# The opening of a hybrid trunk kernel: six blocks of S5's input per piece instead of four

## The chip, the cores and the metric

The kernel runs on one core of a Trainium2 chip. The metric is the device time of one execution in microseconds (us); three runs of the kernel before gave 919.19 us as their median, 918.78 and 919.51 us as the ends. The core has five engines with a queue of their own each, worked off in order: TensorE (PE; its weight loads are listed as PEld), VectorE (DVE), ScalarE (ACT), GpSimd (POOL) and SyncE (SP), which here does little but issue DMAs. They meet through semaphores. A DMA may be issued by SP, by ACT or by POOL.

## The reference

One layer of a decoder trunk with 256 positions and a model width of 2048. The part that matters here is the normalisation, the input projection and what the S5 branch takes from it:

```python
def hybrid_layer(x, mem, pre_g, ...):
    h = rms_norm(x, pre_g)
    proj = h @ w_in
    a_u, a_v, a_g, b_x, b_g, x_q, x_g, gate_logits = jnp.split(proj, splits, axis=-1)
    y_a = spatial_gating(a_u, a_v, sg_ln_g, sg_ln_b, sg_w, sg_b) * jax.nn.silu(a_g)
    y_b = s5_branch(b_x, a_re, a_im, log_dt, b_re, b_im, c_re, c_im, d, glu_w, glu_b) * jax.nn.silu(b_g)
    y_x = memory_cross_attention(x_q, rms_norm(mem, mem_g), xa_wk, xa_wv) * jax.nn.silu(x_g)
    ys = jnp.stack([y_a, y_b, y_x], axis=2)
    branch = jnp.einsum('bsnc,ncd->bsnd', ys, w_branch)
    gates = jax.nn.sigmoid(gate_logits.reshape(bsz, seq, N_BRANCH, D_MODEL))
    merged = jnp.sum(gates * branch, axis=2)
    out = merged @ w_out
    return x + rms_norm(out, post_g)
```

`b_x`, the input of S5, has 1024 columns: eight blocks of 128. Each block is a product of a [2048, 128] strip of `w_in` with `h`, so it is summed over 16 slices of 128 model channels. Everything is in float32.

## The kernel before

Every product is made from two halves of each factor. `split_to` (lines 92 to 94) casts a weight tile to float32r on ACT, the high half `hi`, and subtracts that from the source on DVE, which leaves the low half `lo`; `norm_split` (158 to 167) does the same with a slice of `x`, scaled by the gain `g_pre` on the way. The row's own norm is applied later. `cm_mm` (169 to 174) then issues two matmuls for one block of 128 columns and one slice k: one of 512 columns (the weight's high half against both halves of the slice) and one of 256 columns (the weight's low half against the slice's high half). For the first slice the 512 comes first, for all others the 256.

The program starts with eight matmuls on zeros (`wps`, lines 244 to 247), which belong to no result. Then comes the opening. Eight pieces `pc` hold two slices each, k = 2pc and 2pc + 1. A row of a piece has, for each slice, 256 columns of `x` (transposed) and 512 columns of `w_in`, which are S5's blocks 0 to 3. The first three pieces are loaded slice by slice into the three buffers named `raw`, the others in one DMA each, all of them issued by SP; the very first slice comes as two DMAs, its `x` and its weights. The gains (`vecs`) come by a DMA that ACT issues. For each slice ACT scales (`x`, line 165) and casts (`hl`, line 93), DVE does the two low halves (lines 166 and 94), and PE adds the slice to the four blocks, which lie in two accumulators in PSUM, `acc0[0]` and `acc0[1]` of two banks each. One tile `hl` holds the weight halves of a whole piece, and there are four such tiles in turn (pool `hip`): a cast into a tile has to wait until PE is done with the tile four before it.

After the opening blocks 4 to 7 come as whole strips, each by `cm_block` (line 214): a DMA of 1 MB from `w_bx` into a `raw` buffer, two casts and two subtractions of 1024 columns, 32 matmuls. Blocks 4 and 5 go to two PSUM tiles of the pool `bup` (`b45`), blocks 6 and 7 to a new accumulator from the pool `accp`. That pool has two buffers, so the new one can be written only when an older one has been read out: `fold_u` (lines 338 to 340) adds the two halves of an accumulator into `u`, by a copy on ACT and an addition on DVE.

PE's order is as written in the code. ACT's, DVE's and SP's orders are decided by a scheduler when the kernel is built, from the code, its priorities and its own estimate of when each input is there; on the chip each engine keeps to that order. From line 355 on DVE also builds S5's tables (`tS`), a long row of operations on 32 columns each, which the scheduler fits between the other work.

## Time and profile before

| what | value |
|---|---|
| median of three runs | 919.19 us (918.78 to 919.51) |
| the profiled execution's own time | 919.5 us |
| span of that execution, first to last instruction | 917.8 us |
| DVE busy | 777.1 us, 85% of the span |
| ACT busy | 536.3 us, 58% |
| DMA, mean | 211 GB/s over the span |
| mean granted TensorE clock | 0.998 of full speed |

The execution's own time is 1.7 us more than its span, for what lies before the first and after the last instruction. In a row of the timeline stand the start in us from the span's start, the length in us, the engine, the line, the operation, what is written from what, the shape and how often; in brackets, where there is one, the idle time of the engine ahead of it and what ended that. An engine's next operation can start a little before the one ahead of it has ended. The table of stretches gives for each engine the busy time and the number of instructions, then the clock, the share of time in which the DMA engines are busy, and GB/s.

### The profile page before, as it was taken

To read this page: it belongs to the slowest core of one execution; us is meant where nothing else is said; L and a number is where in the kernel's file an instruction comes from. 1 tells how busy PE (TensorE), PEld (TensorE's weight loads), DVE (VectorE), ACT (ScalarE), POOL (GpSimd) and SP (SyncE) were. 2 spreads that over 40 slices of the span, in tenths; PEclk is the share of its full clock that TensorE was granted. 3 is DMA by queue.
4 is the path that set the end of the run, shared out by engine and by line. 5 is a ranking of instruction groups with operands and counts; after the bars stand their busy time and mean duration, and the time that the engine had idled before them with its cause. 6 is when DMAs were issued, how large, how long until landed. Compare 5 with 4: busy or idle time off the path is not lost.

```text
span 917.8 us, 13203 instructions
## 1 busy us (share of the span) xinstructions
PE 903.1 (98%) x4992; PEld 803.1 (88%) x4992; DVE 777.1 (85%) x1324; ACT 536.3 (58%) x864; POOL 22.6 (2%) x46
## 2 busy tenths in 40 slices
PE   9999999999999999999999999999999999999996
PEld 7999998889888888889999888888888888998896
DVE  7899767968768999999877999999999987876554
ACT  7565755656556666565544656655756646544452
POOL 1000000000000000000000000000000000000000
PEclk9999999999999999999999999999999999999999
DMA  9867765555455556665655555546555666557542
GB/s 350 318 241 281 280 231 190 195 184 195 157 202 179 207 200 221 233 212 184 235 184 184 196 190 198 212 171 210 219 189 189 230 209 209 220 187 276 190 177 92
DMA packets 30464, 193.35 MB, mean 211 GB/s; under 512 B 3904, under 2 KB 4416, under 8 KB 8640
## 3 DMA queue, kind: packets, MB, share of 16 engines
q1 hardware_dynamic: 28288, 186.18, 56.5%
q0 software_dynamic: 1536, 4.20, 1.4%
q10 hardware_dynamic: 576, 2.12, 0.7%
q8 instruction: 39, 0.64, 0.3%
q14 instruction: 25, 0.20, 0.1%
HBM read 190.39 MB, written 2.10 MB: 210 GB/s over the span
## 4 chain that ended last, share of the span: by engine, by line
PE 71%; DVE 19%; ACT 3%; issue 3%; DMA 2%; SPq 0%; DVEq 0%; ACTq 0%
PE acc L182 15%; PE acc L183 15%; PE acc L184 15%; PE acc L172 13%; DVE hl L94 8%; PE acc L171 6%; DVE p L368 3%; ACT hl L93 2%; DVE p L596 2%; DMA raw<-mem 1%; PE acc L179 1%; PE acc L178 1%; PE acc L177 1%; PE po L736 1%; DMA M<-memT 1%
## 5 line engine op out<-in xcount | busy, mean ns | idle before, releaser
L94 DVE TENSOR_TENSOR hl<-raw,hl 128x1024 fp32r<-128x1024 f32 x319 | 388.6, 1221 | 107.0 <-ACT hl L93 103.3
L93 ACT CAST hl<-raw 128x1024 fp32r<-128x1024 f32 x319 | 329.7, 1045 | 185.4 <-PE acc L184 109.4
L172 PE MATMUL acc<-x,hl 128*128 128x512 f32 x736 | 241.2, 383 | 0.0
L171 PE MATMUL acc<-x,hl 128*128 128x256 f32 x690 | 189.4, 275 | 0.8 <-DVE hl L94 0.8
L182 PE MATMUL acc<-hl,x 128*128 128x512 f32 x448 | 171.3, 382 | 0.0
L183 PE MATMUL acc<-hl,x 128*128 128x512 f32 x448 | 169.9, 379 | 0.0
L184 PE MATMUL acc<-hl,x 128*128 128x512 f32 x448 | 169.8, 379 | 0.0
L172 PEld LDWEIGHTS acc<-x,hl 128*128 128x128 f32 x736 | 136.7, 190 | 17.9 <-ACT hl L93 0.9
L171 PEld LDWEIGHTS acc<-x,hl 128*128 128x128 f32 x690 | 132.3, 192 | 3.0 <-DVE hl L94 1.3
L182 PEld LDWEIGHTS acc<-hl,x 128*128 128x128 f32 x448 | 84.7, 189 | 13.2 <-issue 2.1
L184 PEld LDWEIGHTS acc<-hl,x 128*128 128x128 f32 x448 | 84.7, 189 | 12.0
L183 PEld LDWEIGHTS acc<-hl,x 128*128 128x128 f32 x448 | 84.7, 189 | 11.5 <-DVE hl L94 0.2
L182 PE MATMUL acc<-hl,H 128*128 128x512 f32 (+1 forms) x224 | 83.6, 373 | 0.0
L183 PE MATMUL acc<-hl,H 128*128 128x512 f32 (+1 forms) x224 | 83.3, 372 | 0.0
L184 PE MATMUL acc<-hl,H 128*128 128x512 f32 (+1 forms) x224 | 83.2, 372 | 0.0
L182 PEld LDWEIGHTS acc<-hl,H 128*128 128x128 f32 x224 | 42.4, 189 | 5.7 <-ACT E L537 0.4
L183 PEld LDWEIGHTS acc<-hl,H 128*128 128x128 f32 x224 | 42.4, 189 | 5.6 <-DVE hl L94 0.4
L184 PEld LDWEIGHTS acc<-hl,H 128*128 128x128 f32 x224 | 42.4, 189 | 5.5
L368 DVE TENSOR_TENSOR p<-p,E 128x512 f32<-128x512 f32 x64 | 44.0, 688 | 1.0
L537 ACT COPY E<-ebase 128x64 f32<-128x64 f32 x32 | 7.7, 245 | 62.3 <-DVE p L368 58.5
L596 DVE TENSOR_TENSOR_SCAN p<-s5r,p 128x256 f32<-128x256 f32 x64 | 41.7, 680 | 0.8
L368 DVE TENSOR_TENSOR p<-bu,E 128x512 f32<-128x512 f32 x64 | 41.8, 681 | 0.0
(248 smaller groups left out, 1279.1 us busy)
## 6 DMA issues: line engine op xcount, KB each, us to landing
raw<-w_gate SPq DMA_DIRECT2D x48, 1024.0 KB, 4.7
raw<-w_br SPq DMA_DIRECT2D x24, 1024.0 KB, 4.7
raw<-w_out SPq DMA_DIRECT2D x16, 1024.0 KB, 4.7
raw<-w_xq SPq DMA_DIRECT2D x8, 1024.0 KB, 4.8
raw<-wk SPq DMA_DIRECT2D x8, 1024.0 KB, 4.8
raw<-wv SPq DMA_DIRECT2D x8, 1024.0 KB, 4.8
raw<-w_xg SPq DMA_DIRECT2D x8, 1024.0 KB, 4.8
raw<-w_av SPq DMA_DIRECT2D x8, 1024.0 KB, 4.8
```

Source lines behind the costliest of these rows:

```text
L93: a.copy(out=hi, in_=src)
L94: v.tensor_tensor(out=lo, in0=src, in1=hi.bitcast(F32), op=ALU.subtract)
L171: pe.matmul(ps[:, 0:T], lhsT=wl, rhs=hl.moving(0), start=False, stop=False)
L172: pe.matmul(ps, lhsT=wh, rhs=hl.moving_both(), start=first, stop=last)
L177: pe.matmul(ps[:, 0:T], lhsT=wh, rhs=hl.moving(0), start=first, stop=False)
L178: pe.matmul(ps[:, 0:T], lhsT=wh, rhs=hl.moving(1), start=False, stop=False)
L179: pe.matmul(ps[:, 0:T], lhsT=wl, rhs=hl.moving(0), start=False, stop=last)
L182: pe.matmul(ps, lhsT=hl.stationary(0, tb), rhs=two(wh), start=first, stop=False)
L183: pe.matmul(ps, lhsT=hl.stationary(0, tb), rhs=two(wl), start=False, stop=False)
L184: pe.matmul(ps, lhsT=hl.stationary(1, tb), rhs=two(wh), start=False, stop=last)
L368: v.tensor_tensor(out=o, in0=i0, in1=i1, op=op)
L596: v.tensor_tensor_scan(out=p2[:, ri], data0=rb, data1=p1[:, ri], initial=0.0, op0=ALU.mult, op1=ALU.add)
```

## The change

The opening takes blocks 0 to 5 instead of 0 to 3. A slice of a piece now has 256 columns of `x` and 768 of weights, so that its row is full at 1024. The accumulators of blocks 4 and 5 (`b45`) are taken before the opening. After it only blocks 6 and 7 are left of `w_bx`, and the new accumulator for them is the first thing that PE writes.

The first DMAs are cut in another way. One tensor `xvecs` holds the first slice of `x` and all the gains, and SP loads it by one DMA (152 KB). The first slice's weights come by two DMAs that ACT issues, 256 columns (128 KB) and 512 columns (256 KB). SP's second DMA is the second slice (512 KB). The weight halves of the first slice are made in three chunks of 128, 256 and 384 columns, those of the second in two of 384, all others at once with 768. Each slice has a tile `hl` of its own, so four tiles are now four slices.

```diff
-    vecs = const.tile([P, 48 + VPAD], F32, name="vecs")[:, 0:48]
-    nc.scalar.dma_start(out=vecs, in_=I["vecs"])
+    const.tile([P, 32], F32, name="vpad")
+    vecs = xv[:, T:T + 48]
+    first = rawp.tile([P, 2, 1024], F32, tag="raw", name="first")
+    nc.sync.dma_start(out=xv, in_=I["xvecs"])
+    nc.scalar.dma_start(out=first[:, 0, T:T + 256], in_=I["start"][0][:, 0, T:T + 256])
+    nc.scalar.dma_start(out=first[:, 0, T + 256:1024], in_=I["start"][0][:, 0, T + 256:1024])
...
+    b45 = [bup.tile([P, 512], F32, tag="bu", name=f"bx{i}") for i in (4, 5)]
+    ps0 = [acc0[b // 2][:, b % 2] for b in range(4)] + b45
     for pc in range(8):
-        if pc < 3:
-            raw = rawp.tile([P, 2, 768], F32, tag="raw", name=nm("st"), padded_shape=[P, 2, 1024])
+        if pc == 0:
+            raw = first
+        elif pc < 3:
+            raw = rawp.tile([P, 2, 1024], F32, tag="raw", name=nm("st"))
         else:
-            raw = slot(("H0", "H1", "H2", "H3", "M0")[pc - 3], [P, 2, 1024])[:, :, 0:768]
-        wh, wl = (z.rearrange("p (q n) -> p q n", q=2) for z in halves(CM_OFF))
+            raw = slot(("H0", "H1", "H2", "H3", "M0")[pc - 3], [P, 2, 1024])
         parts = [slice(0, 1), slice(1, 2)]
         for q in parts if pc < 3 else [slice(0, 2)]:
-            if pc == 0 and q.start == 0:
-                nc.sync.dma_start(out=raw[:, q, 0:T], in_=I["start"][pc][:, q, 0:T])
-                nc.sync.dma_start(out=raw[:, q, T:768], in_=I["start"][pc][:, q, T:768])
+            if pc > 0 or q.start > 0:
+                nc.sync.dma_start(out=raw[:, q], in_=I["start"][pc][:, q])
+        for k in range(2):
+            kk = 2 * pc + k
+            wh, wl = halves(CM_OFF)
+            norm_split(xv[:, 0:T] if kk == 0 else raw[:, k, 0:T], g_pre, xhl[kk:kk + 1], kk)
+            if kk == 0:
+                chunks = [slice(0, 128), slice(128, 384), slice(384, 768)]
+            elif kk == 1:
+                chunks = [slice(0, 384), slice(384, 768)]
             else:
-                nc.sync.dma_start(out=raw[:, q], in_=I["start"][pc][:, q])
...
+                chunks = [slice(0, 768)]
+            for c in chunks:
+                split_to(wh[:, c], wl[:, c], raw[:, k, T + c.start:T + c.stop])
+            for b in range(6):
+                ws = slice(b * P, (b + 1) * P)
+                cm_mm(ps0[b], wh[:, ws], wl[:, ws], xhl[kk], kk == 0, kk == 15)
...
-    b45 = [bup.tile([P, 512], F32, tag="bu", name=f"bx{i}") for i in (4, 5)]
-    cm_block(b45[0], load(I["w_bx"][0]), xhl)
+    ps = acc_tile()
+    raw0 = load(I["w_bx"][0])
     for i in range(2):
         fold_u(u[:, 2 * i:2 * i + 2, :], acc0[i])
-    cm_block(b45[1], load(I["w_bx"][1]), xhl)
-    ps = acc_tile()
-    cm_block(ps[:, 0], load(I["w_bx"][2]), xhl)
     for i in range(2):
         fold_u(u[:, 4 + i, :], b45[i])
+    cm_block(ps[:, 0], raw0, xhl)
...
-    cm_block(ps[:, 1], load(I["w_bx"][3]), xhl)
+    cm_block(ps[:, 1], load(I["w_bx"][1]), xhl)
```

The scheduler lays the work out anew. ACT's queue at the start, before (line, operation, written from read; `x_110` and `x_111` are the first two slices, `hl_130` the first piece's weight halves, `st_129` its raw data; what a row waits for stands in brackets, a name with DMAHW being a DMA):

```order
L118 DMA vecs<-vecs 128x48
L116 ACT_TABLE_LOAD
L116 ACTIVATE warm<-warm 128x1 [waits Pool_49]
L165 ACTIVATE x_110<-st_129,vecs 128x2x128 [waits DMAHW1_49,DMAHW0_49]
L93 CAST hl_130<-st_129 128x512 [waits DMAHW2_49]
L165 ACTIVATE x_111<-st_129,vecs 128x2x128 [waits DMAHW3_49]
L93 CAST hl_130<-st_129 128x512
```

And now, where `x_113` and `hl_135` are the first slice, `x_114` and `hl_156` the second, DMAHW2 is SP's 512 KB for the second slice and DMAHW3 the second DMA that ACT issues:

```order
L120 DMA first<-start 128x256
L115 ACT_TABLE_LOAD
L115 ACTIVATE warm<-warm 128x1 [waits Pool_49]
L121 DMA first<-start 128x512
L168 ACTIVATE x_113<-xv 128x2x128 [waits DMAHW1_49]
L92 CAST hl_135<-first 128x128 [waits DMAHW0_49]
L168 ACTIVATE x_114<-first,xv 128x2x128 [waits DMAHW2_49]
L92 CAST hl_156<-first 128x384
L92 CAST hl_135<-first 128x256 [waits DMAHW3_49]
L92 CAST hl_135<-first 128x384
L92 CAST hl_156<-first 128x384
```

The second slice's scaling and its first cast now stand ahead of the first slice's second and third chunk; DVE has the same order.

DVE's queue at the end of the opening, before (`hl_323` is the last piece of the opening, `hl_365` and `hl_384` are the two halves of block 4's strip, `hl_409` is the first half of block 5's, `acc_127` and `acc_128` are the opening's accumulators):

```order
L94 TENSOR_TENSOR hl_323<-M_18_322,hl_323 128x512 [waits Activation_49]
L94 TENSOR_TENSOR hl_365<-raw_363,hl_365 128x1024 [waits DMAHW5_49,Activation_49]
L94 TENSOR_TENSOR hl_384<-raw_363,hl_384 128x1024 [waits Activation_49]
L340 TENSOR_TENSOR U_126<-acc_127,U_126 128x512 [waits Activation_49]
L340 TENSOR_TENSOR U_126<-acc_128,U_126 128x512 [waits Activation_49]
L94 TENSOR_TENSOR hl_409<-raw_407,hl_409 128x1024 [waits DMAHW6_49,Activation_49]
```

And now, where `hl_412` is the last slice of the opening, `hl_452` and `hl_471` are the two halves of block 6's strip, `hl_495` is the first half of block 7's, and the accumulators are `acc_130` and `acc_131` (the lines of dots leave out table operations on 32 columns, and nothing else):

```order
L93 TENSOR_TENSOR hl_395<-M_24_393,hl_395 128x768 [waits Activation_49]
...
L93 TENSOR_TENSOR hl_412<-M_24_393,hl_412 128x768 [waits Activation_49]
...
L93 TENSOR_TENSOR hl_452<-raw_442,hl_452 128x1024 [waits DMAHW5_49,Activation_49]
...
L93 TENSOR_TENSOR hl_471<-raw_442,hl_471 128x1024 [waits Activation_49]
...
L93 TENSOR_TENSOR hl_495<-raw_493,hl_495 128x1024 [waits DMAHW1_49,Activation_49]
L349 TENSOR_TENSOR U_129<-acc_130,U_129 128x512 [waits Activation_49]
L349 TENSOR_TENSOR U_129<-acc_131,U_129 128x512 [waits Activation_49]
```

The additions that empty the accumulators have moved behind a third strip half, `hl_495`, and table operations have come in between: 11 ahead of `hl_412`, 8 ahead of `hl_452`, 8 ahead of `hl_471` and 11 ahead of `hl_495`, 38 in all. Nine of them, seven behind `hl_412` and two behind `hl_452`, are one chain on the same column, each using what the one ahead has written.

PE at the end of the opening, before (`x_125` is the last slice, `bx_361` the accumulator of block 4):

```order
L171 MATMUL acc_128<-x_125,hl_323 128x256
L172 MATMUL acc_128<-x_125,hl_323 128x512
L172 MATMUL bx_361<-x_110,hl_365 128x512 [waits Activation_49]
L174 MATMUL bx_361<-x_110,hl_365 128x256 [waits DVE_49]
L171 MATMUL bx_361<-x_111,hl_365 128x256
```

And now (`x_128` is the last slice, `bx_133` the accumulator of block 5, `acc_441` that of block 6):

```order
L174 MATMUL bx_133<-x_128,hl_412 128x256
L175 MATMUL bx_133<-x_128,hl_412 128x512
L175 MATMUL acc_441<-x_113,hl_452 128x512 [waits DVE_49]
L177 MATMUL acc_441<-x_113,hl_452 128x256
L174 MATMUL acc_441<-x_114,hl_452 128x256
```

Where block 4 followed the opening in a tile of its own, block 6 follows now in `acc_441`, which takes the place of `acc_130` in PSUM, and its first matmul waits for DVE.

More of the change, by code (lines that the diff above doesn't have):

```diff
@@ L36 @@
 NWARM = 8
-VPAD = 112
 CM_OFF = 352 // 4
@@ L49, in trunk @@
     xp = ctx.enter_context(tc.tile_pool(name="xp", bufs=1))
-    xp.tile([P, 96], F32, name="xpad")
+    xv = xp.tile([P, T + 48], F32, name="xv")
     const = ctx.enter_context(tc.tile_pool(name="const", bufs=1))
@@ L258, in trunk @@
         parts = [slice(0, 1), slice(1, 2)]
         for q in parts if pc < 3 else [slice(0, 2)]:
-            if pc == 0 and q.start == 0:
-                nc.sync.dma_start(out=raw[:, q, 0:T], in_=I["start"][pc][:, q, 0:T])
-                nc.sync.dma_start(out=raw[:, q, T:768], in_=I["start"][pc][:, q, T:768])
-            else:
-                nc.sync.dma_start(out=raw[:, q], in_=I["start"][pc][:, q])
-        for q in parts:
-            for k in range(q.start, q.stop):
-                norm_split(raw[:, k, 0:T], g_pre, xhl[2 * pc + k:2 * pc + k + 1], 2 * pc + k)
-            split_to(wh[:, q], wl[:, q], raw[:, q, T:768])
-            for k in range(q.start, q.stop):
-                for b in range(4):
-                    ws = slice(b * P, (b + 1) * P)
-                    kk = 2 * pc + k
-                    cm_mm(acc0[b // 2][:, b % 2], wh[:, k, ws], wl[:, k, ws], xhl[kk], kk == 0, kk == 15)
+            if pc > 0 or q.start > 0:
+                nc.sync.dma_start(out=raw[:, q], in_=I["start"][pc][:, q])
@@ L1065, in chv @@
         return z.reshape(-1, 128).T
-    o["vecs"] = np.ascontiguousarray(np.concatenate(
-        [chv(f["pre_norm_g"][0]), chv(f["mem_norm_g"][0]), chv(f["ssm_d"][0].reshape(-1)), chv(f["glu_b"][0])], axis=1))
+    o["xvecs"] = np.ascontiguousarray(np.concatenate(
+        [x.T[:128], chv(f["pre_norm_g"][0]), chv(f["mem_norm_g"][0]), chv(f["ssm_d"][0].reshape(-1)), chv(f["glu_b"][0])], axis=1))
     w = f["w_in"][0]
@@ L1073, in layouts @@
             o["start"] = np.ascontiguousarray(np.concatenate(
-                [x.T.reshape(8, 2, 128, 256), c[:, :512].reshape(8, 2, 128, 512)], axis=3).transpose(0, 2, 1, 3))
-            c = c[:, 512:]
+                [x.T.reshape(8, 2, 128, 256), c[:, :768].reshape(8, 2, 128, 768)], axis=3).transpose(0, 2, 1, 3))
+            c = c[:, 768:]
         o[n] = tm(c) if n == "w_av" else cm(c)
```

## The prediction

> **What bounds the kernel.** The page's first part comes first, then what PE waited for over the whole span (us in total, times, longest).
>
> ```profile
> PE 903.1 (98%) x4992; PEld 803.1 (88%) x4992; DVE 777.1 (85%) x1324; ACT 536.3 (58%) x864; POOL 22.6 (2%) x46
> PE acc L171 <- ACT H L93: 1.4, 1, 1.4
> PE tp L726 <- DVE p L720: 1.1, 1, 1.1
> PE acc L174 <- DVE hl L94: 1.0, 2, 0.7
> PE acc L171 <- DVE hl L94: 0.8, 1, 0.8
> PE acc L179 <- DVE hl L94: 0.7, 1, 0.7
> ```
>
> PE works 903.1 of 917.8 us. The change leaves its matmuls as they are in number and shape, so only PE's waits can move the time, one for one. Of those listed only the 0.8 lies in the opening; the four others, 4.2 us together, stand outside the opening.
>
> The timeline of the first 8 us, all engines:
>
> ```profile
> 1.42 3.60 PE L247 MATMUL wps<-wz 128*128 128x512 bf16 x8 [1.42 <-POOL wz L244]
> 3.22 0.51 ACT L165 ACTIVATE x<-st,vecs 128x256 fp32r<-128x256 f32 x1 [0.47 <-DMA vecs<-vecs]
> 4.36 0.62 ACT L93 CAST hl<-st 128x512 fp32r<-128x512 f32 x1 [0.64 <-DMA st<-start]
> 5.03 0.73 PE L172 MATMUL acc<-x,hl 128*128 128x512 f32 x1
> 6.09 0.51 ACT L165 ACTIVATE x<-st,vecs 128x256 fp32r<-128x256 f32 x1 [1.11 <-DMA st<-start]
> 6.63 0.48 DVE L166 SCALAR_TENSOR_TENSOR x<-st,vecs,x 128x256 fp32r<-128x256 f32 x1 [0.93 <-ACT x L165]
> 7.14 0.69 DVE L94 TENSOR_TENSOR hl<-st,hl 128x512 fp32r<-128x512 f32 x1
> 7.46 0.51 ACT L165 ACTIVATE x<-st,vecs 128x256 fp32r<-128x256 f32 x1 [0.35 <-DMA st<-start]
> 7.89 0.38 PE L171 MATMUL acc<-x,hl 128*128 128x256 f32 x1 [0.77 <-DVE hl L94]
> 12.43 0.38 PE L172 MATMUL acc<-x,hl 128*128 128x512 f32 x1
> 12.75 0.38 PE L172 MATMUL acc<-x,hl 128*128 128x512 f32 x1
> ```
>
> A pair of matmuls takes 12.75 - 12.43 = 0.33 us, a slice of four blocks 1.31 us. At 7.89, where the second slice starts, PE has done one slice; it has **lost 7.89 - 1.31 = 6.58 us**, and from there no row of PE shows a wait until the end of S5's input.
>
> **The start.** The chunks of the first slice let its first matmul start sooner, but PE's warm-up matmuls stand ahead of it and end at 1.42 + 3.60 = 5.02, where block 0 starts already. That gains nothing. What counts is when PE can run on. ACT now does the second slice's scaling and first cast before the first slice's second chunk, so after block 0 PE waits for the second slice's DMA, call its landing L. Bytes and speeds of before:
>
> ```profile
> st<-start SPq DMA_DIRECT2D x5, 384.0 KB, 5.9
> st<-start SPq DMA_DIRECT2D x1, 256.0 KB, 3.1
> st<-start SPq DMA_DIRECT2D x1, 128.0 KB, 2.2
> vecs<-vecs ACTq DMA_DIRECT2D x1, 24.0 KB, 2.4
> 10.00:12.00 2.00, 2.00 (x14) 1.81 (x13) 2.00 (x5) 1.58 (x4) 0.00 (x0) 1.00 1.03 416
> 0.81 0.41 ACTq L118 DMA_DIRECT2D vecs<-vecs  x1
> 2.54 0.20 ACT L116 ACTIVATE warm<-warm 128x1 f32<-128x1 f32 x1
> ```
>
> ACT's waits above give the landings: 128 + 24 KB by 3.22, 256 more by 4.36, 384 more (792 KB in all) by 6.09, 1176 KB by 7.46. Now 152 + 128 + 512 KB, again 792, come up to the second slice if ACT's 256 KB stays out of its way: L = 6.09. If that is served wholly ahead, 1048 KB lie before L, and between the two landings L = 6.09 + 256/384 x 1.37 = 7.00. I take the middle, **L = 6.5**. The ends: everything at the later 416 GB/s from 3.0 on (0.81 + 2.2), 640 KB in 1.6 us, L = 4.6; and the next landing, 7.46.
>
> The Trainium skill, page "DMA: Bandwidth & Descriptors", section "Issuing engines are not separate DMA queues", says that DMAs from different engines interleave on the same 16 DMA engines and that a second issuer saves only issue time. By it L would be 7.0 and the sum 0.5 us higher; in the trace of before only the 24 KB of `vecs` shared the start with SP, too little to tell.
>
> ACT could issue the 256 KB between 1.25 (its first issue ends 0.81 + 0.41) and 2.74 (the warm row's end). With the 3.1 us of the 256 KB row they land by 4.4 to 5.8, ahead of L + 0.82, where ACT asks for them; that choice costs nothing.
>
> From L on, the rows that price ACT and DVE:
>
> ```profile
> 12.44 0.51 ACT L165 ACTIVATE x<-H,vecs 128x256 fp32r<-128x256 f32 x1 [0.86 <-DMA H<-start]
> 12.86 0.60 ACT L93 CAST hl<-H 128x512 fp32r<-128x512 f32 x1
> 13.37 0.50 ACT L165 ACTIVATE x<-H,vecs 128x256 fp32r<-128x256 f32 x1
> 13.49 0.69 DVE L94 TENSOR_TENSOR hl<-H,hl 128x512 fp32r<-128x512 f32 x1
> 14.10 0.48 DVE L166 SCALAR_TENSOR_TENSOR x<-H,vecs,x 128x256 fp32r<-128x256 f32 x1
> 32.32 1.22 DVE L94 TENSOR_TENSOR hl<-raw,hl 128x1024 fp32r<-128x1024 f32 x1
> 33.15 1.05 ACT L93 CAST hl<-raw 128x1024 fp32r<-128x1024 f32 x1 [1.57 <-PE bx L172]
> ```
>
> Scaling holds ACT 0.42 us (12.44 to 12.86). A cast is 0.60 us at 512 columns and 1.05 at 1024, so by the line through both 0.49 at 384, 0.38 at 256, 0.83 at 768; the next starts 0.09 earlier (12.86 + 0.60 against 13.37). The second slice's cast of 384 starts at L + 0.42, the first slice's of 256 at L + 0.82. DVE starts 0.54 after L (6.09 to 6.63) and subtracts from L + 1.05 (7.14). A subtraction is 0.69 at 512, 1.22 at 1024, so 0.56 at 384, 0.43 at 256, 0.95 at 768, the next 0.08 earlier. The first slice's 256 columns begin at L + 1.53 and are there at L + 1.96; with PE's step of 0.05 PE runs on from L + 2.0. By then it has done block 0 and block 1's 512-column matmul, two thirds of a pair, 0.55 us in all. What it needs next (ACT and DVE want 1.2 and 1.4 us a slice, the DMA 1.26 at 416 GB/s) comes faster than PE's 6 x 0.327 = 1.96. Lost: 6.5 + 2.0 - 0.55 = 7.95, against 6.58: **+1.4 us**. It breaks even at L = 5.13. The ends give -0.5 and +2.3.
>
> **The end of the opening.** Block 6 writes the buffer of `acc_130`, so PE waits until DVE has added it up. Before, two strips lay between. DVE's two additions of before, then its small operations: the eight of a chain, up to the next row, and the rows that head and close a stretch of 14 others (38.91 to 40.41):
>
> ```profile
> 27.88 1.34 DVE L340 TENSOR_TENSOR U<-acc,U 128x512 f32<-128x512 f32 x2 [0.41 <-ACT U L339]
> ...
> 35.87 1.76 DVE L371 SCALAR_TENSOR_TENSOR tS<-tS 128x32 f32<-128x32 f32 x8
> 37.67 0.19 DVE L368 TENSOR_TENSOR tS<-tS 128x32 f32<-128x32 f32 x1
> 38.91 0.18 DVE L365 TENSOR_SCALAR tS<-tS 128x32 f32<-128x32 f32 x1
> ...
> 40.41 1.22 DVE L94 TENSOR_TENSOR hl<-raw,hl 128x1024 fp32r<-128x1024 f32 x1
> ```
>
> One costs 1.50/14 = 0.11 us, in the chain 1.80/8 = 0.225; an addition 1.34/2 = 0.67. Let S be where PE starts the last slice. Slice 14's cast needs the tile of slice 10, which PE leaves at S - 4 x 1.96 = S - 7.86; with 0.2 for the last matmul's end, 0.83 for the cast and 0.05 to DVE, its subtraction starts at S - 6.8. From there to the end of `acc_130`'s addition stand two subtractions of 768 (0.87 each to the next start), three of 1024 (1.14), the addition (0.67), together 5.83, and 38 small operations, 9 in the chain: 9 x 0.225 + 29 x 0.11 = 5.2. That ends at S - 6.8 + 11.0 = S + 4.2; PE is through the last slice at S + 1.96. **+2.3 us.** With the small operations free, ACT sets it: the cast of `hl_495` needs slice 14's tile, S + 0.2, then 1.05, a subtraction 1.14 and the addition 0.67 end at S + 3.1, +1.2 us. With half of the 29 in chains too (14 x 0.115 more), +3.9.
>
> Nothing else moves PE: the halves of blocks 6 and 7 are made by then, their strips are loaded long before (the 8.4 MB of the opening take 20 us at 416 GB/s, S lies near 37), and later orders change by a few places.
>
> The sum is +3.7 us on the profiled execution's own 919.5 us (span 917.8), 923.2; that execution is 0.3 above the median of 919.19, so **922.9 us**.
>
> **Rivals.** (a) The opening does what it is cut for and the addition is as early as ACT allows: L = 4.6 and +1.2, 919.19 - 0.5 + 1.2 = 919.9. For it: the DMA engines stream at 416 GB/s two microseconds later. Against: 792 KB took until 6.09, and 38 small operations stand in DVE's queue. (b) PE's clock falls in the gap after block 0. It runs from about 5.7 to L + 1.25 = 7.75. The last 11.8 us of the span:
>
> ```profile
> 906.00:917.80 11.80, 3.82 (x35) 3.63 (x33) 6.50 (x14) 0.77 (x3) 0.00 (x0) 0.82 0.46 178
> ```
>
> PE ends at 909.8; a mean of 0.82 is 4.2 us at half speed, so the clock fell 3.8 us after PE stopped. The gap here is 2.1 us, and would reach 3.8 only at L above 8. If it fell, the return to full speed would cost about half of the 3.6 us that the eight warm-up matmuls took, +1.8: 924.7. The Trainium skill, page "TensorE: Matmul & The Clock Gate", section "Part 1: The HAM clock gate", has the clock drop after one idle window of about 3.4 us that runs freely; the 3.8 us here agree, and by it too this gap is short of one. (c) On the other side: S5's tables are begun earlier, and DVE, ahead by the time PE stood still, removes later waits of PE on DVE, 1.1 + 1.0 + 0.7 = 2.8 us. With (a) that is 919.9 - 2.8 = 917.1, faster; it needs all three to go and L below 5.13. Against: those waits lie far behind, and each follows work that PE itself set off.
>
> **How the numbers follow.** Forecast with both waits, 922.9: chance 0.72, its own range 921.1 to 925.3. (a) 0.16, (b) 0.08, (c) 0.04. About 0.2% (1.84 us) is what a measurement of this kernel can tell from no change: below 917.35 is faster, above 921.03 slower. Slower has the forecast and (b), 0.80; within has (a), 0.16, and half of (c), 0.02; faster the rest, 0.02. The range goes from 920.3, part of the way to (a), to 925.4, past (b) and the forecast's upper end.
>
> **What would show it.** In the changed profile: PE's block 0 near 5.0, then a wait of 1.5 to 3 us on ACT's cast ended by the second slice's DMA near 6.5; a second wait of 2 to 3 us near 41 us on DVE's line 349; the clock at full share between 6 and 10. A wait of the first kind under 0.5 us, or none at the first matmul of block 6, would make the forecast wrong.

## The result and the profile after

| | before | after |
|---|---|---|
| median | 919.51 us (918.78 to 920.34) | 922.90 us (921.56 to 926.33) |
| ratio after / before | | 1.0043, 95% interval 1.0033 to 1.0053 |
| span of the profiled execution | 917.8 us | 921.5 us (its own time 923.24 us) |

The changed kernel is slower by 0.43%, 3.4 us by the medians. The forecast was 922.9, with 0.80 on slower. The number came out; three of its terms did not, as the sections below show.

First the row of busy times of the changed kernel, then what PE waited for over its whole span (us in total, times, longest):

```profile
PE 904.1 (98%) x4992; PEld 804.2 (87%) x4992; DVE 777.6 (84%) x1323; ACT 536.3 (58%) x863; POOL 22.1 (2%) x46
```

```profile
PE acc L175 <- DVE U L349: 2.1, 1, 2.1
PE acc L175 <- ACT hl L92: 2.0, 1, 2.0
PE acc L174 <- ACT H L92: 1.4, 1, 1.4
PE tp L733 <- DVE p L727: 1.1, 1, 1.1
PE acc L177 <- DVE hl L93: 1.0, 2, 0.7
```

The two waits at the head are new and are the two that the forecast named. What is gone against before are the 0.7 us behind line 179 and the 0.8 us of the opening. PE's busy time has grown by 1.0 us, though it does the same 4992 matmuls: some ran slower.

The start, in the timeline of the changed kernel:

```profile
1.25 1.28 ACT L115 ACT_TABLE_LOAD   x1 [1.25 <-PEq L1122]
1.32 0.39 ACTq L121 DMA_DIRECT2D first<-start  x1
...
5.19 0.27 PE L177 MATMUL acc<-x,hl 128*128 128x256 f32 x1
...
6.21 0.51 ACT L168 ACTIVATE x<-first,xv 128x256 fp32r<-128x256 f32 x1 [1.79 <-DMA first<-start]
...
7.47 0.48 PE L175 MATMUL acc<-x,hl 128*128 128x512 f32 x1 [2.01 <-ACT hl L92]
8.09 0.58 PE L177 MATMUL acc<-x,hl 128*128 128x256 f32 x1
8.47 0.63 PE L175 MATMUL acc<-x,hl 128*128 128x512 f32 x1
```

The second slice landed at 6.21; ACT had stood 1.79 us for it, with the first slice's second chunk behind it in its queue. PE ran on at 8.09, 1.88 us after the landing. The second slice (SP, issued at 1.25) and the chunks' 256 KB (ACT, issued at 1.32) took, from issue to landing, in us (the last number):

```profile
first<-start SPq DMA_DIRECT2D x1, 512.0 KB, 4.9
first<-start ACTq DMA_DIRECT2D x1, 256.0 KB, 5.0
```

So the two landed together, at 6.2 and 6.3 us. Behind the wait a matmul of 512 columns takes 0.63 us instead of 0.38. The table of stretches says why (the columns as in before; the granted clock is the third number from the end):

```profile
7.00:8.00 1.00, 0.48 (x1) 0.19 (x1) 1.00 (x4) 1.00 (x4) 0.00 (x0) 0.91 1.01 389
8.00:9.00 1.00, 0.91 (x3) 0.82 (x4) 1.00 (x4) 1.00 (x3) 0.00 (x0) 0.50 1.00 340
9.00:10.00 1.00, 1.00 (x5) 0.91 (x4) 0.96 (x2) 1.00 (x3) 0.00 (x0) 0.50 0.92 361
10.00:12.00 2.00, 2.00 (x10) 1.76 (x10) 2.00 (x4) 1.68 (x3) 0.00 (x0) 0.69 1.07 446
```

The clock fell to half at 7.8 and came back at 11.2 us. The end of the opening, DVE and then PE:

```profile
40.98 1.22 DVE L93 TENSOR_TENSOR hl<-raw,hl 128x1024 fp32r<-128x1024 f32 x1
42.12 1.28 DVE L349 TENSOR_TENSOR U<-acc,U 128x512 f32<-128x512 f32 x2
...
42.85 0.48 PE L175 MATMUL acc<-x,hl 128*128 128x512 f32 x1 [2.08 <-DVE U L349]
```

The addition that frees the accumulator stands behind the strip half `hl_495` on DVE, and PE waits for it as forecast.

To see where time goes behind these waits, the start of PE's n-th matmul was set against the start of the n-th in before, in the profiled executions (matmuls on zeros are not counted). This **lag** is in us; the columns are named by where that matmul starts in before, and the rows of the experiments belong to the next section.

| kernel | 10.7: first slices done | 38.2: block 6 starts | 66.0 | 88.0 | 117.3 | end | median over that of before | ratio, 95% interval |
|---|---|---|---|---|---|---|---|---|
| after | 2.42 | 4.66 | 4.77 | 4.77 | 3.42 | 3.69 | +3.39 | 1.0033 to 1.0053 |
| a_other_banks | 2.46 | 2.46 | 2.46 | 2.46 | 2.39 | 2.62 | +2.04 | 1.0014 to 1.0032 |
| c_keep_warm | 0.62 | 2.88 | 2.98 | 2.98 | 1.58 | 1.77 | +1.90 | 1.0015 to 1.0032 |
| g_tables_late | 3.28 | 4.73 | 4.83 | 4.83 | 4.62 | 4.55 | +3.46 | 1.0024 to 1.0046 |
| j_tables_early | 1.85 | 4.69 | 4.80 | 4.80 | 3.78 | 4.06 | +3.69 | 1.0026 to 1.0051 |
| b_one_queue | 1.88 | 3.96 | 4.06 | 4.86 | 4.38 | 4.34 | +3.65 | 1.0032 to 1.0056 |
| q_dma_first | -0.24 | 1.73 | 1.83 | 3.06 | 3.44 | 3.40 | +4.61 | 1.0035 to 1.0061 |
| e_old_start | 1.91 | 3.66 | 7.17 | 7.49 | 9.36 | 9.36 | +5.15 | 1.0036 to 1.0064 |
| f_four_blocks | 0.37 | 0.37 | 0.37 | 0.78 | 0.80 | 0.75 | +0.04 | 0.9995 to 1.0012 |
| d_banks_and_queue | 0.05 | 0.15 | 0.15 | 2.69 | 2.10 | 2.01 | +2.54 | 1.0020 to 1.0044 |
| n_banks_warm_tables | 0.67 | 0.67 | 0.67 | 2.21 | 1.86 | 2.09 | +0.89 | 1.0001 to 1.0019 |
| i_banks_warm | 0.49 | 0.49 | 0.49 | 0.49 | 0.45 | 0.61 | +0.97 | 1.0003 to 1.0021 |
| s_banks_order_warm | -0.14 | -0.14 | -0.14 | 2.00 | 0.87 | 0.80 | +0.79 | 0.9998 to 1.0016 |

For the changed kernel: 2.4 us are lost at the start, 2.2 at block 6, and 1.3 come back between 88 and 117 us.

### The profile page after: what moved, and what is told of

It reads as the page before. It is cut to its first block, busy times and chain, and to the rows that moved or that the text cites. A ratio compares the mean times of both kernels' runs of the same rounds, so it can differ in the third digit from the quotient of the medians.

```text
span 921.5 us, 13201 instructions
## 1 busy us (share of the span) xinstructions
PE 904.1 (98%) x4992; PEld 804.2 (87%) x4992; DVE 777.6 (84%) x1323; ACT 536.3 (58%) x863; POOL 22.1 (2%) x46
## 4 chain that ended last, share of the span: by engine, by line
PE 79%; DVE 15%; ACT 3%; issue 2%; DMA 1%; DVEq 0%; SPq 0%; ACTq 0%
PE acc L175 16%; PE acc L185 15%; PE acc L187 15%; PE acc L186 15%; PE acc L174 8%; DVE hl L93 5%; DVE p L375 3%; PE acc L182 2%; PE acc L180 2%; PE acc L181 2%; DVE p L603 2%; ACT hl L92 1%; PE po L743 1%; PE acc L177 1%; PE y L627 1%
## 5 line engine op out<-in xcount | busy, mean ns | idle before, releaser
L93 DVE TENSOR_TENSOR hl<-raw,hl 128x1024 fp32r<-128x1024 f32 x315 | 384.1, 1221 | 105.0 <-ACT hl L92 101.4
L92 ACT CAST hl<-raw 128x1024 fp32r<-128x1024 f32 x315 | 325.7, 1045 | 183.2 <-PE acc L187 108.3
```

Source lines behind the costliest of these rows:

```text
L92: a.copy(out=hi, in_=src)
L93: v.tensor_tensor(out=lo, in0=src, in1=hi.bitcast(F32), op=ALU.subtract)
```

## The experiments

All edits are to the changed kernel. Where results are compared with before, they are compared with runs of it on the same chip.

### Block 6's wait

**Banks of their own.** Blocks 6 and 7 go to two PSUM tiles that are free at that time.

```diff
-    ps = acc_tile()
+    ps67 = [miscp.tile([P, 512], F32, tag="misc", name="bx6"), yp.tile([P, 512], F32, tag="y", name="bx7")]
...
-    cm_block(ps[:, 0], raw0, xhl)
+    cm_block(ps67[0], raw0, xhl)
...
-    cm_block(ps[:, 1], load(I["w_bx"][1]), xhl)
-    fold_u(u[:, 6:8, :], ps)
+    cm_block(ps67[1], load(I["w_bx"][1]), xhl)
+    for i in range(2):
+        fold_u(u[:, 6 + i, :], ps67[i])
```

> Blocks 6 and 7 of S5's input go to two PSUM banks of their own instead of the accumulator pair that still holds blocks 0 to 3; each is folded by itself. Theory (the 2.1 us wait of TensorE at block 6 is for the addition that frees that pair, which stands behind the split and the small table operations on VectorE): that wait falls to the 0.2 us or less by which the block's weights are late, and the run is 2.3 us shorter than after, about 920.6 us. Rival 1 (VectorE is simply behind, and the cast of the block's weights is late by as much): the wait stays near 2 us and only changes its name to the cast, time as after, 922.9. Rival 2 (the 1.2 us that TensorE won back later, between 96 and 118 us, came from VectorE's getting ahead while TensorE stood still): the wait goes, but the later return goes with it, 921.8. The start is untouched: the two waits before 8.1 us stay, and the clock falls there as in after.

Measured: 921.70 us (920.26 to 923.15), 2.04 over before. The wait is gone, the lag stays at 2.46 through block 6, and nothing comes back later: rival 2. PE's waits between 44 and 150 us, in before and in this run:

```profile
PE acc L179 <- DVE hl L94: 0.7, 1, 0.7
```

```profile
PE acc L182 <- DVE hl L93: 1.0, 2, 0.7
```

The changed kernel has no PE row there. Its weight loads (PEld) wait 0.5 us in that stretch, those of before 1.5 and of this run 1.6:

```profile
PEld acc L182 <- DVE hl L93: 0.5, 3, 0.2
```

So of these three runs the one in which PE was held at block 6 while DVE went on is without the waits on DVE near 115 us, which before has too. The wait at block 6 costs 2.2 us there and 1.1 at the end (lags 3.69 and 2.62).

**The tables later.** The DMAs of `sp` and `Cin` move behind the fold of blocks 6 and 7.

```diff
-    nc.sync.dma_start(out=sp, in_=I["s5p"])
-    for i in range(2):
-        nc.sync.dma_start(out=Cin[i], in_=I["s5c"][:, i])
     cm_block(ps[:, 1], load(I["w_bx"][1]), xhl)
     fold_u(u[:, 6:8, :], ps)
+    nc.sync.dma_start(out=sp, in_=I["s5p"])
+    for i in range(2):
+        nc.sync.dma_start(out=Cin[i], in_=I["s5c"][:, i])
```

> After, with the inputs of S5's tables loaded behind the folds of blocks 6 and 7 instead of ahead of block 7's weights. VectorE then has 17 to 18 small table operations in front of the addition that frees the accumulators for block 6, instead of 38, and one large subtraction fewer stands in between. It tells what the wait at block 6 is made of. Theory (38 small operations, worked out as 5.2 us, and the strip half ahead of the addition make it): the wait at block 6 falls from 2.1 us to between 0 and 1.2; VectorE does the small ones later, where TensorE is not waiting for them, and the 1.2 us that came back in after between 93 and 117 us shrink by what TensorE no longer stands still: 921.8 to 922.6. Rival 1 (the wait is VectorE's total backlog, and the small operations only move): the wait falls, but TensorE waits as much later on, 922.9 or a little over. Rival 2 (as when the tables came early: the scheduler fills VectorE up to the addition with whatever it has): the wait stays over 1.8 us, 922.9. The start is as in after.

Measured: 923.04 us (921.07 to 924.43), 3.46 over before; PE loses 1.45 us at block 6 (lag 3.28 to 4.73). The last steps, ACT, DVE and PE:

```profile
39.70 1.05 ACT L92 CAST hl<-raw 128x1024 fp32r<-128x1024 f32 x1 [0.92 <-PE bx L175]
```

```profile
41.05 1.22 DVE L93 TENSOR_TENSOR hl<-raw,hl 128x1024 fp32r<-128x1024 f32 x1
42.18 1.28 DVE L349 TENSOR_TENSOR U<-acc,U 128x512 f32<-128x512 f32 x2
```

```profile
42.92 0.48 PE L175 MATMUL acc<-x,hl 128*128 128x512 f32 x1 [1.29 <-DVE U L349]
```

ACT's cast waits for PE to leave a tile, and the subtraction and the addition follow. That is the floor of 1.2 us that the forecast had for the case that the small operations cost nothing. With 17 of them left it is 1.45, with 38 it was 2.24: they are worth 0.8 us of it. Nothing of that was won: the return behind 88 us fell from 1.35 to 0.2. Rival 1 has it: the operations moved, and PE's waits with them. (The profiled execution also had a slower start, of which the last section tells.)

**The tables earlier.** `sp` (48 KB) is loaded ahead of the fifth piece.

```diff
     for pc in range(8):
...
+        if pc == 4:
+            nc.sync.dma_start(out=sp, in_=I["s5p"])
...
-    nc.sync.dma_start(out=sp, in_=I["s5p"])
```

> After, with the 48 KB of inputs of S5's tables (sp) loaded by SyncE ahead of the fifth piece instead of behind block 6's weights; VectorE then does some 60 of the small table operations between the slices' subtractions, where it stood idle for about 30% of 14 to 30 us. Theory (from 31 to 97 us VectorE is the engine that sets TensorE's pace; the small operations, which began at 32.4 us in after, are its backlog): VectorE is 4 to 6 us earlier behind the opening, the wait at block 6 falls from 2.1 us to 1.2 us or less (the strip half ahead of the addition stays), the waits between 85 and 125 us go, and the lag behind before at the end is 0.5 to 2.2 us instead of 3.7: 920.0 to 921.7. Rival 1 (VectorE sets nothing after 45 us, and the 1.2 us returned for another reason): the gain is at the wait of block 6 alone, 921.9 to 922.9. Rival 2 (the small operations come in the way of the slices' subtractions, and TensorE waits inside the opening): slower than after, over 923.2. The start is as in after, with the clock's fall in some executions.

Measured: 923.61 us (922.15 to 924.66), 3.69 over before: no gain, and the theory fell. DVE did do table operations in the opening (its busy share between 14 and 30 us rose from 10.96 us of 16 to 14.17), but the wait at block 6 grew to 2.7 us, since the scheduler filled DVE up to the addition with operations further down the list. DVE's total work is not what sets that wait; its order is.

### The clock

**Kept busy.** Eight more matmuls on zeros behind block 0 of the first slice.

```diff
                 cm_mm(ps0[b], wh[:, ws], wl[:, ws], xhl[kk], kk == 0, kk == 15)
+                if kk == 0 and b == 0:
+                    for _ in range(8):
+                        pe.matmul(wps, lhsT=wz[:, 0:P], rhs=wz, start=True, stop=True)
```

> Eight matmuls of 512 columns on the zeros of the warm-up (they belong to no result) follow block 0 of the first slice on TensorE; everything else is as in after. Theory (the granted clock fell at 7.9 us because TensorE stood still from 5.46 to 7.47, and matmuls at half the clock cost 1.5 us until 11 us): the eight fill that gap, the granted clock stays at full share between 7 and 12 us, block 1 begins no later than in after, and the run is 1.5 us shorter, 921.4 us; if the clock was also what made after's runs differ (921.6 to 926.3), they now lie within 1.5 us. Rival (the clock falls there whatever TensorE does, because only the share of the work in the first 8 us counts, or it falls later instead): time as after, 922.9, with the low share between 7 and 11 us again or moved behind 9 us. Beside them: if the eight matmuls run past 7.5 us (each 0.22 to 0.43 us), they delay block 1 by up to 1.4 us, and the gain is used up.

Measured: 921.56 us (921.05 to 923.58), 1.3 less than after by the medians. PE ran on at full speed, the lag behind the first slices fell from 2.42 to 0.62, and all else stayed as it was (block 6 costs 2.26, 1.4 come back from 88 us to 117). The theory held: half-speed matmuls at the start are a term of 1.3 to 1.5 us. Of the 1.8 us by the lags 0.3 belong to the second slice, which landed at 5.9 here. The runs still spread over 2.5 us, more than the 1.5 expected, which speaks against the clock as the only thing in which the runs of the changed kernel differ.

### The order at the start

**One queue.** The first slice's 512 columns are issued by SP, between `xv` and the second slice.

```diff
-    nc.scalar.dma_start(out=first[:, 0, T + 256:1024], in_=I["start"][0][:, 0, T + 256:1024])
+    nc.sync.dma_start(out=first[:, 0, T + 256:1024], in_=I["start"][0][:, 0, T + 256:1024])
```

> The second of the first DMAs of ScalarE (512 columns of the first slice's weights, 256 KB) is issued by SyncE between xv and the second slice. Theory (at the start TensorE waits because ScalarE's order puts the second slice's scaling, which needs a DMA that lands at 6.2 us, ahead of the first slice's second cast): with this edit ScalarE does the first slice's casts first, TensorE's blocks 1 to 5 begin near 6.0 us instead of 7.5, it stands still for under 1 us after block 0, the granted clock does not fall between 7.9 and 11 us, and the loss at the start is 5.5 to 6.2 us instead of 7.5 plus 1.5 of clock. The wait at block 6 stays at 2 us. In all 2.5 to 3.2 us shorter than after: 919.7 to 920.4. Rival (the transfers themselves are the limit: a DMA on SyncE's queue is issued 0.5 to 1 us later and lands with the second slice): the chunk lands near 6.2 us too, TensorE goes on near 7.5 as before, the clock falls as before, 922.9.

Measured: 923.31 us (923.20 to 925.48), 3.65 over before, neither the theory nor the rival. Blocks 1 to 5 did begin early, at 5.57, and the clock stayed, as the theory said; but the second slice landed only at 8.66, 2.45 us later than in after, and PE stood still 2.50 us behind block 5. In the run with banks and queue, with the same DMAs in the same order, it landed at 7.02. Why the two differ stays open. The experiment changes order and transfer together and doesn't tell them apart; the next one does.

**The same transfers, another order.** The small Sigmoid goes behind ACT's two DMAs in the code.

```diff
-    a.activation(out=warm, in_=warm, func=AF.Sigmoid)
...
     nc.scalar.dma_start(out=first[:, 0, T + 256:1024], in_=I["start"][0][:, 0, T + 256:1024])
+    a.activation(out=warm, in_=warm, func=AF.Sigmoid)
```

> After with one line moved: the small Sigmoid that loads ScalarE's table stands behind ScalarE's two first DMAs in the program instead of ahead of them. The transfers stay on their queues and in their order; what changes is the order that follows on ScalarE and VectorE: the first slice's three chunks come ahead of the second slice's scaling. Theory (TensorE's 2 us wait at 5.5 us is the order on ScalarE, which stands waiting for the second slice): the second slice lands near 6 us as in after, but blocks 1 to 5 begin near 5.6 us, TensorE stands still for less than 1.3 us before the second slice, the clock does not fall, and when the first two slices end TensorE is level with before (lag 0 to 0.3 us, where after has 2.4 with the clock's fall). The wait at block 6 stays at 2.1 us. Further on ScalarE has its first cast of the gathered rows (B from sb) one strip later than in after, as in the run with one queue, where 0.8 us was lost between 70 and 93 us: 921.0 to 922.2. Rival 1 (the chunk's own transfer is late, not the order): blocks 1 to 5 begin near 7 us again, and the time is that of after or of keep-warm, 921.6 to 922.9. Rival 2 (what the start gains is wholly taken back at the cast from sb): 922.5 to 923.5.

Measured: 924.19 us (922.23 to 925.60), 4.61 over before. The start, ACT's cast of the chunk and PE's block 1:

```profile
6.04 0.82 ACT L92 CAST hl<-first 128x256 fp32r<-128x256 f32 x2 [1.65 <-DMA first<-start]
...
6.49 0.48 PE L175 MATMUL acc<-x,hl 128*128 128x512 f32 x1 [1.07 <-ACT hl L92]
```

The chunk landed just before 6.04, later than the 5.6 expected. PE went on 0.5 us behind its landing; in after it landed at 6.3, and PE went on 1.1 to 1.2 us later. So the order makes 0.6 to 0.7 of after's wait of 2.0 us, and the rest is the transfer (rival 1). Together with the clock that was enough: PE came out of the first slices 0.24 us ahead of before, the best start of all runs. None of it arrived at the end. Rival 2 comes nearest, though the median lies above its 922.5 to 923.5: 2.0 us went at block 6, 1.2 between 66 and 88, 0.4 more by 117. Its median is 1.2 us above its own profiled execution (922.94); what happened in the others isn't seen.

### Each part alone

**Six blocks with the old first DMAs and whole casts.**

```diff
-    nc.sync.dma_start(out=xv, in_=I["xvecs"])
-    nc.scalar.dma_start(out=first[:, 0, T:T + 256], in_=I["start"][0][:, 0, T:T + 256])
-    nc.scalar.dma_start(out=first[:, 0, T + 256:1024], in_=I["start"][0][:, 0, T + 256:1024])
+    nc.scalar.dma_start(out=vecs, in_=I["xvecs"][:, T:T + 48])
+    nc.sync.dma_start(out=first[:, 0, 0:T], in_=I["start"][0][:, 0, 0:T])
+    nc.sync.dma_start(out=first[:, 0, T:1024], in_=I["start"][0][:, 0, T:1024])
...
-            if kk == 0:
-                chunks = [slice(0, 128), slice(128, 384), slice(384, 768)]
-            elif kk == 1:
-                chunks = [slice(0, 384), slice(384, 768)]
-            else:
-                chunks = [slice(0, 768)]
+            chunks = [slice(0, 768)]
```

> One part of the change alone: six blocks per piece and the end of the opening as in after, but the first DMAs as before the change (the scales on ScalarE's queue; the first slice's columns of x and its 768 columns of weights one after the other on SyncE's), and no slice is cast in chunks. Theory (the 0.96 us and the fall of the clock at the start come from the second slice's work in front of the first slice's second chunk, with TensorE standing still for 2 us): here ScalarE casts the first slice whole before it touches the second, block 0 begins later (5.6 to 6.5 us) but the six blocks run through, the second slice follows within 0.5 us, the clock does not fall, and the loss at the start is 6.2 to 7.0 us: TensorE is 1.5 to 2.5 us ahead of after when the first slice ends. The wait at block 6 stays (2 us), and VectorE is as late near 97 us as in the experiment with banks and queue (a lag of at least 2.1 us behind before): 921.3 to 922.4. Rival 1 (VectorE sets nothing later on): the whole gain of the start stays, 920.4 to 921.4. Rival 2 (six blocks per piece cost as much whatever the first DMAs): as after, 922.9.

Measured: 925.07 us (923.46 to 928.91), 5.15 over before: none of the three. Its profile is of its slowest execution, 928.91 us, so what follows is larger than in the median. The start lost 1.91 us, the clock's fall included, which the theory had excluded. Then PE lost 3.5 us near 60 and 1.9 near 110. The first of these can be followed back. SP, POOL, ACT and DVE of this run:

```profile
38.99 0.33 SPq L78 DMA_DIRECT2D raw<-w_xq  x1
39.37 0.43 SPq L338 DMA_DIRECT2D M<-memT  x1
```

```profile
50.43 1.21 POOL L517 DMA_DIRECT2D sb<-s5b  x2
```

```profile
57.18 0.40 ACT L529 CAST B<-sb 128x256 fp32r<-128x256 f32 x1 [4.58 <-DMA sb<-s5b]
```

```profile
59.96 1.23 DVE L93 TENSOR_TENSOR hl<-raw,hl 128x1024 fp32r<-128x1024 f32 x1 [5.21 <-ACT hl L92]
```

The same four of the run with banks and matmuls on zeros (below), where nothing is lost:

```profile
32.96 0.33 SPq L346 DMA_DIRECT2D M<-memT  x1
37.99 4.96 SPq L78 DMA_DIRECT2D raw<-w_xq  x2
```

```profile
41.39 1.21 POOL L526 DMA_DIRECT2D sb<-s5b  x2 [0.19 <-POOL sb L525]
```

```profile
45.74 0.71 ACT L538 CAST B<-sb 128x256 fp32r<-128x256 f32 x2
```

Read from the top: in this run SP's order has a strip of `w_xq` ahead of `memT`, and the load `sb`, which waits for the memory half, is issued 9.0 us later than in the other run (3.2 of them are this run's later start, by the lags at block 6). ACT has the cast of `sb` ahead of a strip's cast in its queue and stands 4.6 us, DVE stands 5.2 us behind it, and PE pays. But the late issue is the smaller part of the wait. ACT came to the cast at 57.18 - 4.58 = 52.60, 2.2 us after the issue. From issue to landing the strip of that time and the two loads `sb` took, in us (the last number), here:

```profile
raw<-w_xq SPq DMA_DIRECT2D x1, 1024.0 KB, 8.3
sb<-s5b POOLq DMA_DIRECT2D x2, 128.0 KB, 7.0
```

and in the run with banks and matmuls on zeros:

```profile
raw<-w_xq SPq DMA_DIRECT2D x1, 1024.0 KB, 4.8
sb<-s5b POOLq DMA_DIRECT2D x2, 128.0 KB, 2.7
```

With 2.7 us ACT would have stood about half a microsecond. The other profiles agree (runs are named by their first letters in the table). In `b`, `d`, `g`, `q` and `s` the load that ACT waits for took 4.8 to 6.4 us, and ACT stands 2.8, 2.5, 1.8, 3.2 and 2.9 us; in `f` it took 4.1, and ACT stands 1.0; in before, after, `a`, `c`, `i`, `j` and `n` the first of the loads took 2.3 to 3.7, and ACT does not stand for it. SP's order does not separate them: before and `f` have strips of `w_xq` ahead of `memT` as well, and `g` and `s` have `memT` first. What made the loads slow stays open.

What such a wait costs can be read from DVE. Of the 48 us from 44 to 92 DVE is busy 47.75 to 47.91 in before, after, `a`, `c`, `f` and `i`, 47.07 in `g` and 46.65 in `j`. In these the lag grows by at most 0.1 us from block 6 to 88 us (0.4 in `f`). In `b`, `d`, `e`, `n`, `q` and `s` it is busy 42.70 to 45.71: it stands 2.0 to 5.2 us at a time for a cast that ACT does late because ACT waited for a transfer. There the lag grows by 0.9 to 3.8 us.

**Four blocks with the new first DMAs and chunks.** Before's blocks and end of the opening:

```diff
-            for b in range(6):
+            for b in range(4):
...
-                chunks = [slice(0, 128), slice(128, 384), slice(384, 768)]
+                chunks = [slice(0, 128), slice(128, 384), slice(384, 512)]
```

> The other part alone: before's four blocks per piece and before's end of the opening, with after's first DMAs on two queues and its casts in chunks (with 512 columns the chunks are 128, 256 and 128, then 256 and 256). Theory (the new order at the start costs by when the second slice lands, since its scaling stands ahead of the second chunk on ScalarE): the second slice is 384 KB instead of 512 and lands near 5.6 us, TensorE goes on with block 1 near 7.0 to 7.4 us instead of 7.47, and the loss at the start is 0.2 to 0.7 us over before; where the clock falls in the gap, 1.2 to 1.5 us more. There is no wait at block 6: 919.7 to 921.3. Rival 1 (the first DMAs gain what they look made for: block 0 at 4.9 us instead of 5.03 and no waiting): 919.0 to 919.4. Rival 2 (the transfers start late whatever their size): lands near 6.2 us as in after, 920.6 without a fall of the clock, 922 with one.

Measured: 919.96 us (919.52 to 921.70), 0.04 over before, no difference that can be told, and within the theory's range. The second slice landed at 5.03, PE's wait for the chunk was 0.7 us, and the start lost 0.37. The new first DMAs by themselves neither cost nor gain more than the interval allows (0.5 us less to 1.1 more); the loss comes with the six blocks.

### Parts put together

**Banks and one queue** (the first and the fifth edit above).

> The edits of the first two experiments together: the 256 KB on SyncE's queue, and blocks 6 and 7 in banks of their own. Theory (the wait at block 6 and ScalarE's order at the start, with the fall of the clock that follows from it, are separate causes): the gains add up, 2.3 for the banks and 2.5 to 3.2 for the start, so 917.4 to 918.1 us, under the kernel before (919.5). Rival (what TensorE wins in the opening is taken back at the next place where VectorE or a transfer is behind, and the 1.2 us of later return go): 918.6 to 919.5. If the fall of the clock stays because the share of work in the first 8 us is too small anyway, 1.5 more than the theory.

Measured: 922.20 us (921.56 to 926.09), 2.54 over before. PE leaves the opening level with before (0.15) and is 2.69 behind at 88 us, after DVE has stood 2.2 us at 56.6 behind ACT's wait for `sb`: the rival, and more than it said.

**Banks, matmuls on zeros, tables early.**

> After with three edits: blocks 6 and 7 in banks of their own, the eight matmuls on zeros (they belong to no result) after block 0, and the table inputs early. Theory (three separate causes: the clock's fall 1.5 us, the addition at block 6 2.3 us, VectorE's pace from 31 to 97 us, which gave 1.2 us back in after by TensorE's late arrival and takes 2 us where TensorE arrives early): what is left of the loss is the 0.5 to 1 us of the start, and the waits that before itself has near 97 us (2.2 us in all) go too: 917.5 to 919.5, under the kernel before. Rival (the pace from 31 to 97 us is set by the transfers of the strips, or by VectorE's large subtractions alone, which the early tables don't shorten): as in the experiment with the banks alone less the clock, 920.2 to 920.7.

Measured: 920.81 us (919.98 to 922.53), 0.89 over before, 0.1 above the rival's range. The 1.5 us between 83 and 88 us are again an engine that waits in its order for a late transfer (ACT, then DVE behind it):

```profile
84.27 1.06 ACT L299 ACTIVATE raw<-raw 128x1024 f32<-128x1024 f32 x1 [6.38 <-DMA raw<-x]
...
86.39 1.23 DVE L93 TENSOR_TENSOR hl<-raw,hl 128x1024 fp32r<-128x1024 f32 x1 [2.03 <-ACT hl L92]
```

At this place DVE stood idle, so what was lost here is not its pace, which the theory named.

**Banks and matmuls on zeros.**

> After with blocks 6 and 7 in banks of their own and the eight matmuls on zeros (they belong to no result) after block 0; the tables as in after. Theory (causes add up by their places: 2.4 us of start with the clock's fall become 0.6 as in keep-warm; block 6 waits for nothing; nothing comes back between 93 and 117 us, as with the banks alone, where the lag went from 2.46 to 2.62): a lag of 0.7 to 0.9 at the end, 920.2 to 920.6, 0.2 to 0.6 less than with the tables early as well. Rival (the order of ScalarE and VectorE shifts again by edits that are far away, and a cast stands waiting for a late transfer, as it did between 82 and 88 us with the tables early): 920.8 to 921.6. Rival 2 (VectorE has less lead with an earlier TensorE and takes a part back between 60 and 114 us): the same time, but with its waits spread over several strips.

Measured: 920.55 us (919.88 to 921.22), 0.97 over before, lag 0.61 at the end: the theory, and the one run in which the terms simply add up (its order behind the opening is the one of `a`).

**Banks, the Sigmoid behind the DMAs, four matmuls on zeros.**

> The version put together from the parts that helped: the Sigmoid behind ScalarE's first two DMAs (so that the first slice's chunks come first), banks of their own for blocks 6 and 7, and four matmuls on zeros (they belong to no result) after block 0. Theory: the start as before or up to 0.3 us later, no wait at block 6, no fall of the clock, and between 45 and 117 us what the banks alone had (0.2): a lag of 0.2 to 0.5 us, 919.7 to 920.2, which is level with before (919.5 to 919.9). For it to be under before, one of the waits of before itself between 93 and 114 us (1.5 us by the lags) would have to go, and no run has shown that without TensorE standing still ahead of it. Rival (ScalarE's order shifts, a cast waits for a late transfer): 1 to 2 us more, 921 to 922.

Measured: 920.37 us (919.86 to 920.72), ratio 1.0007, interval 0.9998 to 1.0016: just above the 919.7 to 920.2 expected. PE is 0.14 us ahead of before until 66 us, loses 2.1 by 88, and gets 1.1 back. The loss comes after ACT's wait of 2.9 us for `sb`, behind which DVE stands:

```profile
50.59 1.22 DVE L93 TENSOR_TENSOR hl<-raw,hl 128x1024 fp32r<-128x1024 f32 x1 [2.04 <-ACT hl L92]
```

No version was faster than before.

## Why the prediction was right, and where it wasn't

The profiled execution, term by term (its lag at the end is 3.69 us, the forecast 3.7):

| step of the prediction | forecast | measured |
|---|---|---|
| landing of the second slice, L | 6.5 | 6.21 |
| PE runs on at L + | 2.0 | 1.88 |
| start, 0.55 us done by then | +1.4 | 8.09 - 0.55 - 6.58 = +0.96 |
| clock (rival b) | 0, chance 0.08 | 1.5, the rest of the 2.42 |
| block 6 | +2.3 | 4.66 - 2.42 = +2.24 |
| later waits of PE on DVE (rival c) | 0, chance 0.04 | 3.69 - 4.66 = -1.0 |

- **The start: mechanism right, size off by 0.4.** L was taken in the middle of 6.09 and 7.00; it was 6.21, near the lower. The lower end stood for ACT's own 256 KB staying out of the second slice's way, and that is not what happened: they landed beside it, at 6.3, so 1048 KB were there by then, where before had 792 at 6.09. The transfers did share the way, but were faster together than the speeds taken from before. The step from L was 0.12 shorter. That the order on ACT makes PE wait holds for about a third of the 2.0 us: with the other order (`q`) the wait is still 1.07, since the chunk itself lands at 6.0. The forecast's landing for it, 4.4 to 5.8, was too early.
- **The chunks gain nothing: right for this order.** Block 0 started at 4.90 instead of 5.03. With four blocks nothing was won or lost; with `q`'s order PE leaves the first slices earlier than in before, and the gain is gone at block 6 in `q` itself and by 88 us in `s`.
- **The clock: wrong.** The step that failed is "the gap here is 2.1 us, and would reach 3.8 only at L above 8". It took one idle stretch at the end of the span for a threshold. The gap was 2.0 us and the clock fell: of the forecast's signs "the clock at full share between 6 and 10" is the one that did not show. Filling the gap (`c`) brought 1.3 us.
- **Block 6: right.** 2.24 for 2.3, on the engine, line and operations named. Its parts as well: with 17 instead of 38 small operations 1.45, beside a floor of 1.2; without the shared accumulator nothing.
- **"Nothing else moves PE": wrong.** 1.0 us came back, by rival (c)'s mechanism ("DVE, ahead by the time PE stood still"), which was priced only together with a good start. The run `a` shows that it hangs on PE's standing still: without the wait the return is gone. And in the runs `b`, `d`, `e`, `n`, `q` and `s` waits behind the opening took 0.9 to 5.7 us (5.7 in the slowest execution of `e`).

So the forecast's 922.9 stood on two errors that met: 1.5 us of clock not counted, against 0.4 too much at the start and 1.0 that came back. That these cancel to within 0.1 us is luck; that the two waits came where and nearly as long as forecast is not.

## What to carry to other kernels

A wait during which another engine gets ahead can cost less than its length: subtract the later waits that it takes away, and expect them back when it is mended. Where each engine runs a fixed order, look for instructions that need a late transfer and stand ahead of the one that the bound engine waits for; after a small edit at the start such a pair can cost time some 50 us later, so compare the lag of the bound engine along the whole run, and not the place of the edit alone.

## What the runs showed of the hardware

**The clock does not go by the length of a gap alone.** In the changed kernel two stretches of 3.41 us, up to the fall and from there to the return:

```profile
4.41:7.82 3.41, 1.29 (x5) 0.51 (x3) 1.61 (x5) 1.62 (x6) 0.00 (x0) 1.00 1.01 377
7.82:11.23 3.41, 3.27 (x11) 2.77 (x11) 3.37 (x7) 3.13 (x7) 0.00 (x0) 0.50 0.99 381
```

PE was busy 1.29 of the 3.41 us in front of the fall. In `a` and `e` the half-speed spell lasted 3.41 us as well. In `e` PE's longest gap ahead of it was 1.3 us, and PE was busy 1.58 of the 3.41 us:

```profile
4.19:7.60 3.41, 1.58 (x7) 0.78 (x6) 1.23 (x2) 0.83 (x1) 0.00 (x0) 1.00 0.96 340
```

In `b` PE stood still for 2.50 us, longer than in after, and the clock stayed:

```profile
8.44:11.85 3.41, 1.63 (x10) 1.53 (x11) 2.21 (x5) 2.87 (x6) 0.00 (x0) 1.00 1.00 363
```

The Trainium skill, page "TensorE: Matmul & The Clock Gate", section "Part 1: The HAM clock gate", gives a free-running window of 3413 ns; the length of the half-speed spell agrees. That a whole idle window is needed does not: 1.29 and 1.58 us of work were in it. The place of the window in `b` is worked out from its first matmul at full speed, so that the busy share of a window decides, with a limit between 1.58 and 1.63 us, is argued, not shown.

**The clock column can hide a cold start.** In `j_tables_early` the column stands at 1.00 while matmuls run at half speed:

```profile
8.00:9.00 1.00, 1.00 (x4) 0.91 (x5) 1.00 (x3) 1.00 (x2) 0.00 (x0) 1.00 0.92 307
```

```profile
8.15 0.63 PE L175 MATMUL acc<-x,hl 128*128 128x512 f32 x1
8.57 0.42 PE L177 MATMUL acc<-x,hl 128*128 128x256 f32 x1
```

There the clock had not come up at all before 10.4 us; the first matmul at full speed comes between 4.3 and 13.0 us in the profiled executions. In `g_tables_late` it came last, and its lag of 3.28 at the start is the largest. The durations tell it, the column doesn't, so the mean clock can't say how many of after's executions were hit. Two of its ten lie above 926 us; what held them isn't known.

**ACT's queue issues past a table load.** The second DMA went out at 1.32 us, within the load's 1.25 to 2.53, though it stands behind it in ACT's order.
